# Laying out a kernel's on-chip buffers by class: weights at multiples of 128 bytes, streamed operands 64 bytes off

## The chip, the core and the metric

The kernel runs on one core of a Trainium2 chip. The core has a matrix engine (PE), a vector engine (DVE), a scalar engine (ACT), a general engine (POOL), a queue engine that issues the loads (SP), and 16 DMA engines. On-chip memory has 128 partitions; a tile is a range of bytes that is the same in every partition, so a tile's place is one byte address. The metric is device time of one launch in microseconds (us).

## What is computed

A two-layer decoder trunk on 256 positions of width 1024, batch 1, all in float32: a recurrent block and a gated feed-forward block (FFN), then a shared key/value projection, causal attention with 8 heads and a second FFN. Each block has a root-mean-square norm and a shift and scale that are computed from `c`.

```python
def swiglu(h, w_gate, w_up, w_down):
    return (jax.nn.silu(h @ w_gate) * (h @ w_up)) @ w_down

x = x + g_m[:, None, :] * rglru_mixer(h, ...)      # layer 0
x = x + g_f[:, None, :] * swiglu(h, ...)
x = x + g_m[:, None, :] * moba_mixer(h, ...)       # layer 1
x = x + g_f[:, None, :] * swiglu(h, ...)
return rmsnorm(x, final_norm)
```

`D_FF` is 2816, so each FFN has 2 x 176 weight blocks of 128 x 128 for gate and up and 176 for down.

## The kernel before

The weights come in units of up to 128 x 2048 float32, one DMA each, into a `raw` tile. A matrix product is not done in plain float32. Each weight unit is split in two parts of the matrix engine's rounded float32 type: ACT copies `raw` into `whi` (L433), DVE subtracts that from `raw` into `wlo` (L434). The activations are split in the same way into `..._h` and `..._l`. `mm3` then records three matmuls per 128 x 128 block, at L381 (high weights, high activations), L382 (high weights, low activations) and L383 (low weights, high activations). The weight block is the operand that is loaded into the array ahead of a matmul (the trace's PEld), and the activation block, 128 x 256, is the one that streams through it.

In the FFN the first product (`f_p`) has a unit of 16 weight blocks, 48 matmuls, and streams the four pairs of tiles `f_h` and `f_l`, each with two blocks of 256 columns. The second product (`f_d`) streams eleven pairs `f_ah` and `f_al`. The first two blocks of gate and up (`f_g`) are computed ahead of the norm from tiles `f_u_h` and `f_u_l` with 258 columns; in the first FFN they are done in plain float32 (L443), in the second by three matmuls. The products of the recurrent block (`yb`, `wo`), the query and output products of the attention (`qp`, `ao`) are made like `f_p`. The value product (`vp`) has the two roles exchanged: there the weights stream, 512 columns wide, and the activations are loaded.

All tiles that live for a while only are kept in slots. A class has a fixed number of slots of one size: `t1` 18 of 1032 bytes, `t2` 32 of 2048 bytes, `raw`, `whi` and `wlo` 4 each of 8192 bytes, `mraw` 3 of 4096 bytes. Every streamed operand of `mm3` but those with 258 columns (`t1`) is in a `t2` slot. A planner (`Plan.run`) orders the instructions of every engine from costs and ranks that are written in the code, and gives each tile a slot as its first user is placed. The pool places a slot (a tag) in memory when a tile of that tag is asked for the first time, behind all that was placed until then, and each later tile of the tag has the same place. So before, the slots of all classes lie mixed, in the order in which the plan first used them. Since a `t1` slot has 1032 bytes, taken as 1056, each `t1` slot moves what follows by 32 bytes modulo 128.

Of the kernel before, what the change touches and what calls it, by code (L numbers as in the profile page):

```python
# [12 lines left out]
F32 = mybir.dt.float32  # L13
# [5 lines left out]
P = 128  # L19
D = 1024  # L20
S = 256
# [18 lines left out]
CU = 2048  # L40
# [52 lines left out]
class Plan:  # L93
# [175 lines left out]
KN = {  # L269
    "sp": 287, "winf": 400, "conv": 84, "ga": 109, "y": 284, "ypsum": 80, "ex": -650, "rec": -97, "ge": 245,  # L270
    "gm": 181, "wo": 221, "scf": 103, "shf": -189, "x1": 0, "split": 4, "swp": 1178.2266785918575, "scat": 5,
    "shat": 0, "gmat": 1, "win": 600, "tol": 3.6321997149340305e-16, "nn": 5, "nyh": 1, "sqpe": 1, "gnat": 5,
    "fnat0": 1, "md": "sc", "rawn": 4, "wn": 4, "t2n": 32, "t2r": 2,
}
# [37 lines left out]
T1N, T2N, RAWN, WN, MRN = 18, KN["t2n"], KN["rawn"], KN["wn"], 3  # L312
# [5 lines left out]
def build(tc, t):  # L318
    nc = tc.nc
    ctx = ExitStack()  # L320
    with ctx:
        pool = ctx.enter_context(tc.tile_pool(name="sb", bufs=1))
        psum = ctx.enter_context(tc.tile_pool(name="ps", bufs=1, space=bass.MemoryType.PSUM))
        ctx.enter_context(tc.manual_schedule())
        pl = Plan()
        TW = S + 2

        def slots(cls, n, w, reserve=None, pool=pool):

            pl.slots(cls, n, lambda b, i: pool.tile([P, w], b.dt, name=f"{cls}_{b.name}", tag=f"{cls}{i}"), reserve)  # L330

        slots("t1", T1N, TW, 6)
        slots("t2", T2N, 2 * S, KN["t2r"])
        slots("raw", RAWN, CU, None)
        slots("whi", WN, CU)
        slots("wlo", WN, CU)
        slots("mraw", MRN, D)
        slots("ps", 8, 512, 2, psum)

        def own(shape, name):  # L340
# [208 lines left out]
        def normed(xk, rstd, name):  # L549
            n = T1(name)  # L550
            tt(S, lambda: nc.vector.tensor_mul(n.ap[:, :S], xk.ap[:, :S], rstd.ap[:, :S]), (xk, rstd), (n,))
            return n

        def to_h(n, a, sh, abuf, h, j, name):

            f = T1(name)
            act(S, lambda: nc.scalar.activation(f.ap[:, :S], n.ap[:, :S], AF.Identity, bias=sh(), scale=a()),
                (n,) + abuf, (f,), aps=2)
            hi, lo = h
            o = j * S  # L560
            act(S, lambda: nc.scalar.activation(hi.ap[:, o:o + S], f.ap[:, :S], AF.Copy), (f,), ((hi, o),))
            tt(S, lambda: nc.vector.tensor_sub(lo.ap[:, o:o + S], f.ap[:, :S], hi.f[:, o:o + S]), (f, (hi, o)),
               ((lo, o),))
            return f
# [85 lines left out]
        for k in range(KC):  # L650
# [10 lines left out]
            f = to_h(normed(x0[k], rstd0, f"n0_{k}"), lambda k=k: sc0.ap[:, k:k + 1], lambda k=k: sh0.ap[:, k:k + 1],  # L661
                     ((sc0, k), (sh0, k)), h0[k // 2], k % 2, f"h0_{k}")
# [309 lines left out]
        for k in range(KC):  # L972
            n = normed(x2[k], rstd2, f"n2_{k}")
# [256 lines left out]
```

## Time and profile before

| what | value |
|---|---|
| time, median of 3 runs | 629.61 us (628.73 to 631.35) |
| the profiled execution: time | 628.5 us |
| its span, first to last instruction | 626.7 us |
| PE busy | 597.9 us, 95% of the span |
| DVE busy | 472.6 us, 75% |
| ACT busy | 338.0 us, 54% |
| HBM read | 161.14 MB, 259 GB/s over the span |

The span and the time differ by 1.8 us, which lie around the instructions. Shares are means over stages with different limits, so they say little about one stage. Matmuls overlap: one matmul is shown with 283 ns from start to end, while the next one starts 120 ns after it. What a row of matmuls costs is therefore read from the distance of their starts, not from the mean of one.

### The profile page before, as it was taken

Reading aid. Unit: us, or ns where it says so; the run is one execution under the profiler, and the core shown is the slowest. Engines: PE = TensorE matmul, PEld = TensorE weight load, DVE = VectorE, ACT = ScalarE, POOL = GpSimd, SP = SyncE. Lnnn points to the kernel's source line nnn. Section 1 sums busy time; section 2 is a strip of 40 time slices with the busy share of each in tenths; the row PEclk is TensorE's granted clock in tenths of the full one; section 3 lists DMA queues with packets and bytes.
Section 4 is the critical chain, followed back from the end, with each engine's and each line's share of the span. In section 5 each row is a group of like instructions: output and inputs, shape, how many; then the busy total and the mean of one; then the engine's idle time right before and its main releaser. Section 6 shows DMA issues by size and latency. Waiting matters only on the chain.

```text
span 626.7 us, 11500 instructions
## 1 busy us (share of the span) xinstructions
PE 597.9 (95%) x4688; PEld 574.6 (92%) x4688; DVE 472.6 (75%) x718; ACT 338.0 (54%) x485; POOL 35.1 (6%) x68
## 2 busy tenths in 40 slices
PE   3999899998999999999997999997999999999996
PEld 1899778997999999999996999997999999999996
DVE  6898978887988789988756789888997555545542
ACT  5537998627653444253444988766555433333322
POOL 0000000032000000001006000006000000000000
PEclk9999999999999999999998999998999999999999
DMA  8886897687988899998878248885686543445501
GB/s 292 327 339 241 318 391 302 257 319 291 415 311 306 317 332 355 326 332 333 321 282 318 75 164 315 302 315 215 224 319 226 195 174 132 139 145 186 180 1 68
DMA packets 33363, 162.95 MB, mean 260 GB/s; under 512 B 3700, under 2 KB 4893, under 8 KB 23966
## 3 DMA queue, kind: packets, MB, share of 16 engines
q1 hardware_dynamic: 33310, 162.21, 70.1%
q8 instruction: 37, 0.61, 0.4%
q14 instruction: 16, 0.13, 0.1%
HBM read 161.14 MB, written 1.06 MB: 259 GB/s over the span
## 4 chain that ended last, share of the span: by engine, by line
PE 81%; DVE 6%; DMA 5%; issue 2%; ACT 2%; POOL 2%; SPq 0%; DVEq 0%; POOLq 0%; ACTq 0%
PE ps_f_p L382 12%; PE ps_f_p L381 12%; PE ps_f_p L383 12%; PE ps_f_d L382 7%; PE ps_f_d L381 6%; PE ps_f_d L383 6%; PE ps_xb L670 2%; DVE t_xc L702 2%; PE ps_f_g L443 2%; PE ps_yb L381 1%; PE ps_yb L382 1%; DMA raw_sh_f_r<-in_modp 1%; PE ps_qp L382 1%; PE ps_qp L381 1%; PE ps_qp L383 1%
## 5 line engine op out<-in xcount | busy, mean ns | idle before, releaser
L382 PE MATMUL ps_f_p<-t_f_l,whi_f0b_h 128*128 128x256 f32 x320 | 90.6, 283 | 0.0
L381 PE MATMUL ps_f_p<-t_f_h,whi_f0b_h 128*128 128x256 f32 x320 | 90.5, 283 | 0.0
L383 PE MATMUL ps_f_p<-t_f_h,wlo_f0b_l 128*128 128x256 f32 x320 | 90.3, 282 | 0.0
L381 PE MATMUL ps_f_p<-t_f_h,whi_f1b_h 128*128 128x256 f32 x320 | 90.2, 282 | 0.0
L383 PE MATMUL ps_f_p<-t_f_h,wlo_f1b_l 128*128 128x256 f32 x320 | 90.1, 282 | 0.0
L382 PE MATMUL ps_f_p<-t_f_l,whi_f1b_h 128*128 128x256 f32 x320 | 90.1, 282 | 0.0
L434 DVE TENSOR_TENSOR wlo_f1b_l<-raw_f1b_r,whi_f1b_h 128x2048 fp32r<-128x2048 f32 x20 | 45.8, 2289 | 21.7 <-ACT whi_f1b_h L433 21.5
L381 PEld LDWEIGHTS ps_f_p<-t_f_h,whi_f0b_h 128*128 128x128 f32 x320 | 61.1, 191 | 0.0
L382 PEld LDWEIGHTS ps_f_p<-t_f_l,whi_f0b_h 128*128 128x128 f32 x320 | 61.1, 191 | 0.0
L383 PEld LDWEIGHTS ps_f_p<-t_f_h,wlo_f0b_l 128*128 128x128 f32 x320 | 61.1, 191 | 0.0
L382 PEld LDWEIGHTS ps_f_p<-t_f_l,whi_f1b_h 128*128 128x128 f32 x320 | 60.8, 190 | 0.0
L381 PEld LDWEIGHTS ps_f_p<-t_f_h,whi_f1b_h 128*128 128x128 f32 x320 | 60.8, 190 | 0.0
L383 PEld LDWEIGHTS ps_f_p<-t_f_h,wlo_f1b_l 128*128 128x128 f32 x320 | 60.8, 190 | 0.0
L433 ACT ACTIVATE whi_f1b_h<-raw_f1b_r 128x2048 fp32r<-128x2048 f32 x20 | 38.1, 1913 | 27.1 <-issue 19.3
L434 DVE TENSOR_TENSOR wlo_f0b_l<-raw_f0b_r,whi_f0b_h 128x2048 fp32r<-128x2048 f32 x20 | 45.7, 2289 | 9.0 <-ACT whi_f0b_h L433 8.9
L433 ACT ACTIVATE whi_f0b_h<-raw_f0b_r 128x2048 fp32r<-128x2048 f32 x20 | 38.1, 1911 | 22.2 <-issue 19.1
L382 PE MATMUL ps_f_d<-t_f_al,whi_f1c_h 128*128 128x256 f32 x176 | 49.8, 283 | 0.0
L381 PE MATMUL ps_f_d<-t_f_ah,whi_f0c_h 128*128 128x256 f32 x176 | 49.7, 282 | 0.0
L381 PE MATMUL ps_f_d<-t_f_ah,whi_f1c_h 128*128 128x256 f32 x176 | 49.6, 282 | 0.0
L382 PE MATMUL ps_f_d<-t_f_al,whi_f0c_h 128*128 128x256 f32 x176 | 49.6, 282 | 0.0
L383 PE MATMUL ps_f_d<-t_f_ah,wlo_f1c_l 128*128 128x256 f32 x176 | 49.6, 282 | 0.0
L383 PE MATMUL ps_f_d<-t_f_ah,wlo_f0c_l 128*128 128x256 f32 x176 | 49.6, 282 | 0.0
(470 smaller groups left out, 1696.7 us busy)
## 6 DMA issues: line engine op xcount, KB each, us to landing
raw_f0b_r<-in_ffb SPq DMA_DIRECT2D x20, 1024.0 KB, 6.0
raw_f1b_r<-in_ffb SPq DMA_DIRECT2D x20, 1024.0 KB, 5.9
raw_f0c_r<-in_ffc SPq DMA_DIRECT2D x16, 704.0 KB, 6.5
raw_f1c_r<-in_ffc SPq DMA_DIRECT2D x16, 704.0 KB, 4.1
raw_wix<-in_win_x SPq DMA_DIRECT2D x8, 768.0 KB, 7.2
raw_wout_r<-in_wout SPq DMA_DIRECT2D x5, 1024.0 KB, 8.5
raw_wiy_r<-in_win_y SPq DMA_DIRECT2D x4, 1024.0 KB, 7.5
raw_sh_f_r<-in_modp SPq DMA_DIRECT2D x4, 1024.0 KB, 8.3
```

The lines of the kernel that those rows point to most:

```text
L381: nc.tensor.matmul(o, h_, a_, start=start, stop=False, skip_group_check=skip)
L382: nc.tensor.matmul(o, h_, b_, start=False, stop=False, skip_group_check=skip)
L383: nc.tensor.matmul(o, l_, a_, start=False, stop=stop, skip_group_check=skip)
L433: act(n - o, lambda: nc.scalar.activation(hi.ap[:, o:n], raw.ap[:, o:n], AF.Copy), (raw,), (hi,))
L434: tt(n - o, lambda: nc.vector.tensor_sub(lo.ap[:, o:n], raw.ap[:, o:n], hi.f[:, o:n]), (raw, hi), (lo,))
L443: pe(n * 0.0016875 + 0.002, lambda: nc.tensor.matmul(ps.ap[:, c:c + n], lo.ap[:, o:o + w], xh.ap[:, xo:xo + n], start=start, stop=stop, sk ...
L670: pe(0.432, lambda k=k, m=m, c=c, ps=ps, wr=wr, f=f: nc.tensor.matmul(ps.ap[:, c:c + S], wr.ap[:, m * P:(m + 1) * P], f.ap[:, :S], start=( ...
L702: stt(S, lambda m=m, j=j, o=o, tap=tap: nc.vector.scalar_tensor_tensor(x_.ap[:, o], xv()[:, j, tap:tap + S], V("cw", tap * 10 + m), x_.ap[ ...
```

## The change

The slots are placed before anything else, class by class, and the tiles that stay for the whole program follow. For that, `slots` asks the pool once for a tile of each tag; these tiles have no instruction. A tile of 64 bytes, named `shift`, is placed between `mraw` and `t2`.

```diff
         def slots(cls, n, w, reserve=None, pool=pool):
 
             pl.slots(cls, n, lambda b, i: pool.tile([P, w], b.dt, name=f"{cls}_{b.name}", tag=f"{cls}{i}"), reserve)
-
-        slots("t1", T1N, TW, 6)
-        slots("t2", T2N, 2 * S, KN["t2r"])
-        slots("raw", RAWN, CU, None)
+            if pool is not psum:
+                for i in range(n):
+                    pool.tile([P, w], F32, name=f"{cls}_home{i}", tag=f"{cls}{i}")
+
+
         slots("whi", WN, CU)
         slots("wlo", WN, CU)
+        slots("raw", RAWN, CU, None)
         slots("mraw", MRN, D)
+        pool.tile([P, 16], F32, name="shift", tag="shift")
+        slots("t2", T2N, 2 * S, KN["t2r"])
+        slots("t1", T1N, TW, 6)
         slots("ps", 8, 512, 2, psum)
```

In the two built programs every engine has the same instructions in the same order, with the same waits; only line numbers (5 more below the edit) and buffer numbers differ. What differs is where the tiles lie:

| class | address modulo 128, before | now |
|---|---|---|
| `whi` (4 slots) | one at 96, three at 0 | 0 |
| `wlo` (4) | 0 | 0 |
| `raw` (4) | one at 64, three at 0 | 0 |
| `mraw` (3) | 64, 96, 64 | 0 |
| `t2` (32) | three at 64, 29 at 0 | 64 |
| `t1` (18) | 0, 32, 64 or 96 | each as before |
| tiles that stay | 0, 32, 64 or 96 | each as before |

Which tile has which slot is the same in both. Modulo 512 the weight blocks and the streamed blocks have these places: before, the 29 slots and all weight slots but one are at 384, so that the two are 0 apart; now the weights are at 128 and the streamed blocks at 192, so that a weight block lies 64 below its streamed block (448 modulo 512).

Two places in the program are needed further down. In the matrix engine's order, a part of a unit of the second FFN's first product before: `f1_h3` is one of the few streamed tiles in a slot at 64 modulo 128, the others here are at 0, and so are the weights.

```order
L382 MATMUL ps_f1_p31_5348<-t2_f1_l2_5077,whi_f1b31_h_5189 128x256
L383 MATMUL ps_f1_p31_5348<-t2_f1_h2_5055,wlo_f1b31_l_5236 128x256
L381 MATMUL ps_f1_p31_5348<-t2_f1_h3_5079,whi_f1b31_h_5189 128x256
L382 MATMUL ps_f1_p31_5348<-t2_f1_l3_5096,whi_f1b31_h_5189 128x256
L383 MATMUL ps_f1_p31_5348<-t2_f1_h3_5079,wlo_f1b31_l_5236 128x256
```

Nothing moves there; now all these streamed tiles are at 64. The second place is in the products with 258 columns at the start of the second FFN, whose streamed tiles are in `t1` slots. Here the high part `u3_h` is at 448 modulo 512 and the low part `u3_l` at 320, and both weight blocks at 384.

```order
L383 MATMUL ps_f1_g01_4805<-t1_f1_u3_h_4859,wlo_f1a0_l_4705 128x258
L381 MATMUL ps_f1_g02_4810<-t1_f1_u3_h_4859,whi_f1a0_h_4552 128x258
L382 MATMUL ps_f1_g02_4810<-t1_f1_u3_l_4871,whi_f1a0_h_4552 128x258
L383 MATMUL ps_f1_g02_4810<-t1_f1_u3_h_4859,wlo_f1a0_l_4705 128x258
L381 MATMUL ps_f1_g03_4814<-t1_f1_u3_h_4859,whi_f1a0_h_4552 128x258
```

Nothing moves there either, and the `t1` tiles keep their places modulo 128.

## Rows read from the trace of the kernel before

**Rows 1.** The page's chain of work that ended last, shares by engine.

```profile
PE 81%; DVE 6%; DMA 5%; issue 2%; ACT 2%; POOL 2%; SPq 0%; DVEq 0%; POOLq 0%; ACTq 0%
```

**Rows 2.** Busy time by stretch: two of first FFN, attention, two of second FFN.

```profile
core 0: us, PE busy (x) PEld busy (x) DVE busy (x) ACT busy (x) POOL busy (x), PEclk, DMA share, GB/s
156.40:271.50 115.10, 115.10 (x962) 115.06 (x961) 102.31 (x134) 53.63 (x55) 0.00 (x0) 1.00 0.91 336
271.50:330.60 59.10, 59.10 (x498) 58.97 (x497) 43.98 (x53) 23.72 (x21) 2.75 (x3) 1.00 0.86 323
354.00:424.00 70.00, 70.00 (x519) 66.72 (x518) 62.52 (x136) 55.18 (x120) 1.79 (x3) 1.00 0.71 264
442.00:555.30 113.30, 113.30 (x957) 113.30 (x956) 71.90 (x76) 51.48 (x52) 0.00 (x0) 1.00 0.55 197
555.30:618.80 63.50, 63.50 (x536) 63.50 (x534) 30.39 (x35) 22.23 (x23) 0.00 (x0) 1.00 0.34 113
```

**Rows 3.** Groups of instructions: count, then busy us, mean ns, idle before.

```profile
L382 PE MATMUL ps_f_p<-t_f_l,whi_f0b_h 128*128 128x256 f32 x320 | 90.6, 283 | 0.0
L382 PE MATMUL ps_f_d<-t_f_al,whi_f0c_h 128*128 128x256 f32 x176 | 49.6, 282 | 0.0
L381 PE MATMUL ps_ao<-t_oh,whi_wo_h 128*128 128x256 f32 x64 | 18.7, 292 | 0.0
```

**Rows 4.** Timeline of PE (start, us): first matmuls of two successive first-FFN units.

```profile
185.38 0.28 PE L381 MATMUL ps_f_p<-t_f_h,whi_f0b_h 128*128 128x256 f32 x1
...
191.14 0.28 PE L381 MATMUL ps_f_p<-t_f_h,whi_f0b_h 128*128 128x256 f32 x1
```

**Rows 5.** Timeline of PE: second FFN, matmuls with 258 columns.

```profile
435.01 0.28 PE L383 MATMUL ps_f_g<-t_f_u_h,wlo_f1a_l 128*128 128x258 f32 x1
435.13 0.28 PE L381 MATMUL ps_f_g<-t_f_u_h,whi_f1a_h 128*128 128x258 f32 x1
435.24 0.28 PE L382 MATMUL ps_f_g<-t_f_u_l,whi_f1a_h 128*128 128x258 f32 x1
435.37 0.28 PE L383 MATMUL ps_f_g<-t_f_u_h,wlo_f1a_l 128*128 128x258 f32 x1
435.48 0.28 PE L381 MATMUL ps_f_g<-t_f_u_h,whi_f1a_h 128*128 128x258 f32 x1
435.60 0.28 PE L382 MATMUL ps_f_g<-t_f_u_l,whi_f1a_h 128*128 128x258 f32 x1
435.72 0.28 PE L383 MATMUL ps_f_g<-t_f_u_h,wlo_f1a_l 128*128 128x258 f32 x1
```

**Rows 6.** Timeline of PE: second FFN, first product, two pieces.

```profile
472.32 0.29 PE L381 MATMUL ps_f_p<-t_f_h,whi_f1b_h 128*128 128x256 f32 x1
...
473.26 0.28 PE L383 MATMUL ps_f_p<-t_f_h,wlo_f1b_l 128*128 128x256 f32 x1
...
481.61 0.28 PE L381 MATMUL ps_f_p<-t_f_h,whi_f1b_h 128*128 128x256 f32 x1
...
487.24 0.28 PE L381 MATMUL ps_f_p<-t_f_h,whi_f1b_h 128*128 128x256 f32 x1
```

**Rows 7.** Pieces of the chain that ended last: start us, us, what.

```profile
29.51 2.16 PE ps_xb L670 x10
...
129.77 6.49 DMA mraw_mr_sc_f_m__1416<-in_mod
...
354.45 0.23 PE ps_vp L381
```

**Rows 8.** Timeline of DVE, then of PE, near the first FFN's end.

```profile
305.44 1.63 DVE L434 TENSOR_TENSOR wlo_f0c_l<-raw_f0c_r,whi_f0c_h 128x1408 fp32r<-128x1408 f32 x1 [0.48 <-ACT whi_f0c_h L433]
307.45 1.62 DVE L434 TENSOR_TENSOR wlo_f0c_l<-raw_f0c_r,whi_f0c_h 128x1408 fp32r<-128x1408 f32 x1 [0.38 <-ACT whi_f0c_h L433]
...
310.80 0.28 PE L381 MATMUL ps_f_d<-t_f_ah,whi_f0c_h 128*128 128x256 f32 x1
```

**Rows 9.** Waits of ACT from 157 to 330 us: total us, times, longest.

```profile
ACT whi_f0c_h L433 <- DMA raw_f0c_r<-in_ffc: 15.9, 6, 4.4
```

## The prediction

> **What bounds the kernel now.** I read the chain of work first: 81% of the span is PE, no other engine has over 6% [rows 1]. Then the stretches of the trace one by one. In five of them, 421 us together, PE is busy without a gap: 115.10 of 115.10 us, 59.10 of 59.10 and so on [rows 2]. These are the two FFNs and the attention, and in them only the spacing of the matmuls and what feeds PE can matter. DVE is busy 102.31 of 115.10 us in the worst of them and the DMA engines 91%, so neither is at its limit, though both are near it in the first FFN and far from it in the second (71.90 of 113.30 us, and 55%). [...]
>
> A matmul's own duration (283 ns, [rows 3]) is no price, since the next one starts long before it ends. So I take the time between starts. In a unit of the first FFN in which the streamed tiles and all weights are at 0 modulo 128, the 48 matmuls from one unit's first to the next unit's first take 191.14 - 185.38 = 5.76 us, 120.0 ns each [rows 4]. The weight loads fill that time too: PEld is busy 115.06 of 115.10 us [rows 2]. So while one block streams, the next block's weights are read, all the time, from the same memory.
>
> **Does the place matter? Three stretches.** The kernel before has a few tiles elsewhere, so its trace is a small experiment. (a) The piece of the second FFN in which `f1_h3` (at 64) is streamed, with its neighbours at 0: eight steps from 472.32 to 473.26 us, 0.94 us, 117.5 ns each, against 120.0 [rows 6]. (b) A unit of that product whose high weights lie at 96 and which streams `f1_h3` twice: 487.24 - 481.61 = 5.63 us for 48, 117.3 ns [rows 6]. (c) The matmuls with 258 columns on `u3`, the nearest to what the change makes, because there the loaded weights lie 64 below the streamed tile (384 against 448 modulo 512) as all of them will now. The two steps during which the high part streams take 435.24 - 435.01 = 0.23 us and, one cycle later, 435.60 - 435.37 = 0.23 us: 115 ns each. The step during which the low part streams (weights 64 above it) takes 0.13 and 0.12 us. All six take 0.71 us, 118.3 ns [rows 5]. The timeline rounds to 0.01 us, so the 115 is good to some 5 ns.
>
> I conclude that places decide some nanoseconds per matmul, and that the distance of 0 is the worst that occurs over a long stretch: neither (a), (b) nor (c) is above 120 in the mean.
>
> [...]
>
> **The change part by part.** No instruction, wait or queue entry is added, removed or moved, so every term is a duration.
>
> *Matmuls of three with a `t2` tile streaming.* Per FFN, 3 x 320 of `f_p` and 3 x 176 of `f_d`: 1488 [rows 3]. The attention has 3 x 64 for `ao` and as many for `qp`: 384. Now the spacing: a window's count holds about two matmuls that only reach into it, so in the first FFN 115.10 us / 960 = 119.9 ns and 59.10 / 496 = 119.2, together 119.7; in the second 113.30 / 955 = 118.6 and 63.50 / 534 = 118.9, together 118.7 [rows 2]. For the new spacing the ends are 125 ns, the long step of (c), and 108 ns, half of the 216 ns that a plain float32 pass over 256 columns takes (2.16 us for ten, [rows 7]); that the rounded type takes half as long when nothing disturbs it is an estimate. Between them I take 115 ns, the step of (c) at the new distance. First FFN: (119.7 - 115) x 1488 = 7.0 us. Second: (118.7 - 115) x 1488 = 5.5 us. Attention: 4.2 x 384 = 1.6 us, of which I count half, 0.8 us: there DVE is busy 62.52 of 70 us and each head waits for its exponentials. Sum 13.3 us.
>
> *The same matmuls ahead of the first FFN* (`yb`, `wo` and part of `xb`, about 600 matmuls): 0 us. They are covered by loads: the chain goes through a DMA of 6.49 us at 129.77 us, after most of them [rows 7]. Without that cover they would give 600 x 4.5 = 2.7 us.
>
> *What feeds PE in the first FFN.* When PE is faster, weight slots come free earlier and ACT, DVE and SP move up with it, unless the loads are at their limit. In this FFN ACT waits for `raw_f0c` 15.9 us in six waits [rows 9]. The tightest unit has its low weights ready at 305.44 + 1.63 = 307.07 us and its first matmul at 310.80 us [rows 8]: 3.7 us of reserve. By then PE has gained (310.80 - 156.40) / 0.1197 x 4.7 ns = 6.1 us. If no load came earlier, 2.4 us of the gain would be lost; if all did, nothing. DMA is 91% and 86% busy, not full, so I take 0.9 us. What is late next in that case is a `wlo` at the start of a unit of `f_d`. The second FFN has no such limit at 55% and 34% DMA.
>
> *ACT and DVE on other addresses.* Nothing: DVE's split takes 1.63 us in a unit with high weights at 0 and 1.62 us in the next, where they are at 96 [rows 8]. *`vp`*: here weights stream and `t2` tiles are loaded, so the sign of the distance is turned round; a matmul takes 0.23 us for 512 columns [rows 7], and 48 of them change by 0.8 us at most if one goes to the 216 ns of [rows 7] or as far the other way. *`raw` and `mraw` at 0* are places that DMAs write; 0 us, since the FFNs with most of PE's time do not wait for them except as costed above.
>
> Sum: 13.3 - 0.9 = 12.4 us. 628.5 - 12.4 = 616.1 us in the terms of the profiled execution; the median of the runs stands 0.2% above that execution, so 617 us.
>
> **The rivals.**
>
> *Give-back.* The short steps of (c) and the 0.11 to 0.12 us around them may be paid by the long ones: two operands that change their distance drift, and one at a constant distance settles at the mean, some 117.5 ns as in (a) and (b). For it: in (c) 115 never stands alone for more than two steps. Gain (119.2 - 117.5) x 3360 = 5.7 us: 624 us.
>
> *Nothing happens.* The reads are independent, or they fall into step at any constant distance, as they do at 0, where every step of a unit is 0.12 us. Against it: (a) to (c). 629 us, within 3 us. [...]
>
> *Slower.* All matmuls settle in the long step. Place: both FFNs and the attention; price: 125 ns instead of 119.2, 5.8 x 3360 = 19 us, 649 us. It decides as soon as the settled step is above 119.2 ns. For it speaks only that long steps occur at all at a distance of 64, with the other sign; against it that at the new sign four of four steps are about 115.
>
> *More than expected.* The two reads no longer meet at all: 108 ns, (119.2 - 108) x 3360 = 38 us less, less what the first FFN's loads hold back. For it speaks nothing seen; half way, at 112 ns, it would be about 606 us.
>
> **How the numbers follow.** 115 ns and its surroundings (113 to 117): 0.56, 610 to 622 us. Give-back: 0.19. Nothing: 0.13. Slower: 0.06. More: 0.06. The range from 608 to 627 us holds the first two and the edges of "nothing" and "more", about 8 in 10. A measurement of this kernel tells 0.5% (3 us) from no change; the limit is 626.5 us. Faster: 0.56 + 0.06 + nearly all of give-back, 0.80. Same: 0.14. Slower: 0.06.
>
> **What would show it.** In the trace of the changed kernel, 48 matmuls of a unit of `f_p` should take 5.52 us (115 ns each) instead of 5.76, in all units alike, since all distances are equal; the windows of the second FFN should be shorter by some 5.5 us together, with PE still without a gap. The two passes of the split on ACT and DVE should take what they take now. In the first FFN a wait of PE for `wlo_f0c` would show that the loads hold back the gain. A step that stays at 0.12 us throughout makes the prediction wrong in its first term, a step of 0.12 to 0.13 in its sign. A shorter step with an unchanged time would mean that I misread what PE waits for.

## The result, and the profile after

The changed kernel takes 622.93 us (median of 6 executions, 621.48 to 626.17), the kernel before 629.28 us (median of 6 on the same chip). The ratio is 0.9906, with an interval from 0.9885 to 0.9927. The forecast was 617 us with a range from 608 to 627: the direction came out, and about half of the size, 6.4 us by the medians (5.9 by the ratio) instead of 12.4. Here and below a ratio leaves out an execution that lies more than 1.5% above the fastest of its kernel; there are two, in e8_hilo128 and e10_again.

The profiled execution took 623.06 us, with a span of 621.2 us. First the page's chain by engine, then three of its groups of instructions (count, busy us, mean ns, idle before), which answer to [rows 1, 3]:

```profile
PE 80%; ACT 6%; DVE 4%; DMA 4%; POOL 2%; issue 2%; SPq 0%; DVEq 0%; POOLq 0%; ACTq 0%
...
L387 PE MATMUL ps_f_p<-t_f_l,whi_f0b_h 128*128 128x256 f32 x320 | 89.4, 279 | 0.0
L439 DVE TENSOR_TENSOR wlo_f0b_l<-raw_f0b_r,whi_f0b_h 128x2048 fp32r<-128x2048 f32 x20 | 45.7, 2289 | 8.3 <-ACT whi_f0b_h L438 8.3
...
L387 PE MATMUL ps_f_d<-t_f_al,whi_f0c_h 128*128 128x256 f32 x176 | 49.1, 279 | 0.0
```

PE is the chain as before, and a matmul's own duration has gone from 283 and 282 to 279 ns, which is no price. The same stretches as in [rows 2] (busy us and count of each engine, granted clock, DMA share, GB/s):

```profile
core 0: us, PE busy (x) PEld busy (x) DVE busy (x) ACT busy (x) POOL busy (x), PEclk, DMA share, GB/s
156.40:271.50 115.10, 115.10 (x978) 115.07 (x978) 102.75 (x136) 53.68 (x53) 0.00 (x0) 1.00 0.89 333
...
442.00:555.30 113.30, 113.30 (x964) 113.30 (x963) 71.03 (x73) 50.00 (x50) 0.00 (x0) 1.00 0.55 194
```

PE has no gap (115.10 of 115.10 us) and the granted clock is 1.00, as before, and more matmuls fit into the same time: 978 for 962, 964 for 957. The price is in the starts. The timeline of PE, the first matmul of two units in the first FFN and of two in the second:

```profile
182.94 0.28 PE L386 MATMUL ps_f_p<-t_f_h,whi_f0b_h 128*128 128x256 f32 x1
...
188.59 0.28 PE L386 MATMUL ps_f_p<-t_f_h,whi_f0b_h 128*128 128x256 f32 x1
...
471.83 0.28 PE L386 MATMUL ps_f_p<-t_f_h,whi_f1b_h 128*128 128x256 f32 x1
...
477.49 0.28 PE L386 MATMUL ps_f_p<-t_f_h,whi_f1b_h 128*128 128x256 f32 x1
```

48 matmuls take 5.65 and 5.66 us, where [rows 4] have 5.76 and the forecast had 5.52. That is 117.8 ns each. The program's order tells which weight unit a matmul of the trace belongs to: in all 76 units that PE ran through without a break (30 to 48 matmuls, the first six steps left out) the mean step is 117.7 or 117.8 ns. So the term "matmuls of three" was worth (119.7 - 117.8) x 1488 = 2.8 us in the first FFN and (118.7 - 117.8) x 1488 = 1.3 us in the second, not 7.0 and 5.5. (By [rows 2] the 119.7 is rather 119.6, which is 0.1 us of the sum.)

One place of the same trace showed that this is not the whole story. The timeline of PE in the first FFN, around a step of 0.13 us and a break of 0.22 us:

```profile
157.52 0.28 PE L387 MATMUL ps_f_p<-t_f_l,whi_f0b_h 128*128 128x256 f32 x1
157.64 0.29 PE L388 MATMUL ps_f_p<-t_f_h,wlo_f0b_l 128*128 128x256 f32 x1
157.77 0.28 PE L386 MATMUL ps_f_p<-t_f_h,whi_f0b_h 128*128 128x256 f32 x1
157.88 0.28 PE L387 MATMUL ps_f_p<-t_f_l,whi_f0b_h 128*128 128x256 f32 x1
...
158.11 0.28 PE L386 MATMUL ps_f_p<-t_f_h,whi_f0b_h 128*128 128x256 f32 x1
158.22 0.38 PE L387 MATMUL ps_f_p<-t_f_l,whi_f0b_h 128*128 128x256 f32 x1
158.44 0.28 PE L388 MATMUL ps_f_p<-t_f_h,wlo_f0b_l 128*128 128x256 f32 x1
158.56 0.28 PE L386 MATMUL ps_f_p<-t_f_h,whi_f0b_h 128*128 128x256 f32 x1
```

From 157.77 to 158.22 us four steps take 0.45 us, 113 ns each, behind a step of 0.13; then a start comes 0.22 us after the last one, and from there on it is 117.8 ns. The tiles stand at the same distance all the time.

### The profile page after: what moved, and what is told of

The parts are those of the page before. It is cut to its first block, busy times and chain, and to the rows that moved or that the text cites. A ratio compares the mean times of both kernels' runs of the same rounds, so it can differ in the third digit from the quotient of the medians.

```text
span 621.2 us, 11500 instructions
## 1 busy us (share of the span) xinstructions
PE 593.1 (95%) x4688; PEld 569.8 (92%) x4688; DVE 471.9 (76%) x718; ACT 338.1 (54%) x485; POOL 34.9 (6%) x68
## 4 chain that ended last, share of the span: by engine, by line
PE 80%; ACT 6%; DVE 4%; DMA 4%; POOL 2%; issue 2%; SPq 0%; DVEq 0%; POOLq 0%; ACTq 0%
PE ps_f_p L388 12%; PE ps_f_p L386 12%; PE ps_f_p L387 12%; PE ps_f_d L388 6%; PE ps_f_d L386 6%; PE ps_f_d L387 6%; PE ps_xb L675 2%; PE ps_f_g L448 2%; PE ps_yb L386 1%; PE ps_yb L388 1%; PE ps_yb L387 1%; PE ps_qp L388 1%; PE ps_qp L386 1%; PE ps_qp L387 1%; DMA mraw_mr_sc_f_m__1482<-in_mod 1%
```

## The experiments

All kernels are the changed kernel with other places for the slots; the work is the same. I call distance the address of the weights being loaded minus that of the tile that streams, modulo 512; the changed kernel has 448 throughout, that is -64. The trace doesn't show addresses: the distances are those of the places that the program gives to the tiles. By these places one of the 29 slots that the section on the change has at 384 modulo 512 before lies at 256, which is 0 modulo 128 too; of the distances that are 0 modulo 128, the experiments have 0 alone. Each kernel leaves out the `shift` tile and puts tiles without an instruction in front of the slots, by a table of bytes:

```diff
             if pool is not psum:
                 for i in range(n):
+                    if any(PADS.get(cls, ())[i:i + 1]):
+                        pool.tile([P, PADS[cls][i] // 4], F32, name=f"{cls}_pad{i}", tag=f"{cls}_pad{i}")
                     pool.tile([P, w], F32, name=f"{cls}_home{i}", tag=f"{cls}{i}")
...
-        pool.tile([P, 16], F32, name="shift", tag="shift")
```

**e1_flat: the order by class alone, distance 0 throughout.**

```diff
+        PADS = {}
```

> Slots class by class as in the changed kernel, but without the 64 bytes ahead of t2: all weights and all streamed tiles at 0 modulo 128, distance 0 everywhere. Theory A (the spacing is settled by the constant distance of loaded weights and streamed tile): 120.0 ns in every unit of both FFNs, also in those that had 117 to 119 before; 48 matmuls in 5.76 us; time 629 to 632 us, 1% above the changed kernel. Theory B (the placing by class itself, or the alignment of raw and mraw, gave the gain): about 623 us and a spacing below 120. The recurrent part tells more: under A the first FFN starts at 139.5 us as before the change, under B at 137.5 as after it.

Measured: 630.97 us (10 executions), a ratio of 1.0024 to the kernel before, interval 1.0005 to 1.0042. The first matmuls of two successive units of the first FFN, timeline of PE:

```profile
182.61 0.28 PE L387 MATMUL ps_f_p<-t_f_h,whi_f0b_h 128*128 128x256 f32 x1
...
188.37 0.28 PE L387 MATMUL ps_f_p<-t_f_h,whi_f0b_h 128*128 128x256 f32 x1
```

5.76 us for 48, and 119.9 or 120.0 ns in all 76 units without a break. The order by class and the multiples of 128 alone bring no gain; it takes the 64 bytes. One sign of theory B is there all the same: the first FFN starts at 137.58 us, as in the changed kernel (137.45) and not as before (139.55). And 1.6 us of this trace are not the step: from 137 to 157 us the granted clock is 0.91 in the mean, where the changed kernel has 1.00, and the time from the first matmul of `f_g` to that of `f_p` is 18.57 instead of 16.94 us.

**e2_dist32: distances of 0, 32, 64 and 96, one for each pair of weight slots.**

```diff
+        PADS = {'whi': (0, 32, 32, 32), 'wlo': (416, 32, 32, 32), 'raw': (416, 0, 0, 0)}
```

> One trace with four constant distances: the four slot pairs of whi and wlo lie 0, 32, 64 and 96 bytes above the streamed tiles (modulo 512), so that successive units of f_p have these distances in turn. Theory A: each unit settles in a spacing of its own: 120.0 ns at 0, about 118 at 64, 32 and 96 between 116 and 119. Theory C (any distance but 0 gives the same): 117.8 in the three others.

Measured: 625.69 us (one execution). In the FFNs, units at 0 have 119.8 to 120.0 ns. At 32 they have 118.1 to 118.3, with steps from 115 to 123 that repeat. At 96 eleven of 17 have 117.3 to 117.5, one has 118.5, and five have 120.0, among them all four of the first FFN's second product. At 64 there are two values, 117.8 in five units and 113.3 in twelve. Here are the starts of a unit at 64 and of the next, first in the first FFN and then in the second:

```profile
183.28 0.28 PE L387 MATMUL ps_f_p<-t_f_h,whi_f0b_h 128*128 128x256 f32 x1
...
188.94 0.28 PE L387 MATMUL ps_f_p<-t_f_h,whi_f0b_h 128*128 128x256 f32 x1
...
475.12 0.28 PE L387 MATMUL ps_f_p<-t_f_h,whi_f1b_h 128*128 128x256 f32 x1
...
480.58 0.28 PE L387 MATMUL ps_f_p<-t_f_h,whi_f1b_h 128*128 128x256 f32 x1
```

5.66 us and 5.46 us, 117.8 and 113.3 ns (the last unit's 5.46 holds the step into the next distance), with the same distance. So the distance alone doesn't set the step, and neither theory comes out whole. The streamed tiles lie as in e1_flat here, at 0 modulo 128, and only the weights are moved. That 64 gives 117.8 ns this way round too speaks against a rival that e1_flat leaves open, that the place of the streamed tiles by itself decides.

**e3_dist128 and e5_dist128_timed: distances of 448, 64, 192 and 320, all 64 modulo 128.** The two are the same kernel; the second was timed in several executions.

```diff
+        PADS = {'whi': (448, 128, 128, 128), 'wlo': (128, 128, 128, 128), 'raw': (192, 0, 0, 0)}
```

> Four distances that are all 64 modulo 128 but differ modulo 512: 448 (as in the changed kernel), 64, 192 and 320. Theory A with a period of 128 bytes: 117.8 ns in every unit. Theory D (higher address bits or the sign matter, which would explain steps of 115 and 124 ns at plus and minus 64 before): units differ by more than 1 ns, with 64 above 448.

> The kernel of e3 (slot pairs 448, 64, 192 and 320 bytes above the streamed tiles, modulo 512), now timed. Theory H (at 64 modulo 128 the same addresses have two settled steps, 113.3 and 117.8 ns; a stretch that starts in the long one stays there until something disturbs it, and a change of the distance by 128 is such a disturbance): 113.3 ns in nearly all of both FFNs in every execution, 611 to 615 us, ratio 0.972 to 0.978. Theory R (which step is taken is chance at each start): times on several levels between 612 and 624 us.

Measured: 612.92 us, then 612.64 us (6 executions, 611.63 to 614.32), a ratio of 0.9729 to the kernel before, interval 0.9705 to 0.9753. In both traces 67 of the 68 units of the FFNs have 113.3 ns, at every one of the four distances. Here, from e3, are the start of a unit at 448 and that of the next, 5.44 us later:

```profile
172.15 0.28 PE L387 MATMUL ps_f_p<-t_f_h,whi_f0b_h 128*128 128x256 f32 x1
...
177.59 0.28 PE L387 MATMUL ps_f_p<-t_f_h,whi_f0b_h 128*128 128x256 f32 x1
```

That refutes a settled step that belongs to 448, and leaves two readings: a change of distance helps while it lasts, or it tips the row of matmuls into another state that then stays.

**e4_mixed: high and low weights at different distances (0 and 64, 32 and 96).**

```diff
+        PADS = {'whi': (0, 32, 32, 32), 'wlo': (480, 32, 416, 32), 'raw': (480, 0, 0, 0)}
```

> High and low weights of a unit at different distances: 0 and 64, 32 and 96, 64 and 0, 96 and 32 bytes above the streamed tile in the four slot pairs, so that the distance changes within each three matmuls. Theory A: the mean of the two constant distances, weighted two to one, about 118 to 119 ns. Theory E (a change of distance breaks the settled step and gives short steps of 115 that are not paid back): below 117.8 in the mean.

Measured: 624.46 us (one execution), 117.7 to 118.0 ns in all 68 units of the FFNs, although each three changes its distance twice. A change between 64 and 0 or between 32 and 96 does not bring the short step; theory E is refuted, and the mean of theory A is missed where 0 is one of the two distances (120.0 and 117.8, weighted, would be 118.5 to 119.3).

**e6_const320: one distance throughout, 320 instead of 448.**

```diff
+        PADS = {'t2': (192,)}
```

> All weights 320 above the streamed tiles modulo 512, constant, as the changed kernel has 448. Theory H: like the changed kernel, 117.8 ns where a stretch starts so, with 113.3 only behind a break; 620 to 625 us. Theory D (bits above 7 decide, and 448 alone is bad): 113.3 ns in all units, 611 to 615 us.

Measured: 620.53 us (4 executions, 617.40 to 621.88), ratio 0.9846, interval 0.9813 to 0.9879. In the trace, that of the execution with 617.40 us, the first FFN runs at 113.3 ns until a break of 1.1 us at 299.95 us and at 117.8 behind it, and the second FFN at 117.8. One distance, two steps.

**e7_one128: one of the four pairs of weight slots moved by 128.** Three units in four keep 448, the fourth has 64.

```diff
+        PADS = {'whi': (128, 384, 0, 0), 'wlo': (128, 384, 0, 0), 't2': (64,)}
```

> The changed kernel with one of the four slot pairs moved by 128 bytes (distance 448 in three pairs, 64 in one). Theory H: 117.8 ns at the start of an FFN, 113.3 from about the first unit with the moved pair on, and it stays at 113.3 through the units with 448: 612 to 616 us. Theory D: one unit in four at 113.3, the others at 117.8, about 620 us.

Measured: 613.04 us (4 executions, 610.29 to 615.52), ratio 0.9731, interval 0.9692 to 0.9771. Timeline of PE in the first FFN: the first start of an ordinary unit, some starts of the next, which has the moved pair, and the first starts of the two ordinary units behind it:

```profile
166.78 0.28 PE L387 MATMUL ps_f_p<-t_f_h,whi_f0b_h 128*128 128x256 f32 x1
...
171.73 0.28 PE L387 MATMUL ps_f_p<-t_f_h,whi_f0b_h 128*128 128x256 f32 x1
171.84 0.28 PE L388 MATMUL ps_f_p<-t_f_l,whi_f0b_h 128*128 128x256 f32 x1
171.97 0.28 PE L389 MATMUL ps_f_p<-t_f_h,wlo_f0b_l 128*128 128x256 f32 x1
172.09 0.28 PE L387 MATMUL ps_f_p<-t_f_h,whi_f0b_h 128*128 128x256 f32 x1
172.20 0.28 PE L388 MATMUL ps_f_p<-t_f_l,whi_f0b_h 128*128 128x256 f32 x1
172.31 0.28 PE L389 MATMUL ps_f_p<-t_f_h,wlo_f0b_l 128*128 128x256 f32 x1
...
177.19 0.28 PE L387 MATMUL ps_f_p<-t_f_h,whi_f0b_h 128*128 128x256 f32 x1
...
182.63 0.28 PE L387 MATMUL ps_f_p<-t_f_h,whi_f0b_h 128*128 128x256 f32 x1
```

Until 171.73 us the unit's 42 matmuls take 4.95 us, 117.9 ns each. Then the distance changes, three steps take 0.36 us together (171.73 to 172.09), from there they are 113 ns, and PE waits for nothing. The unit from 177.19 us on is back at 448 and keeps 113.3 ns (5.44 us for 48), and so does all that follows in this FFN, with one exception: in `f0_d5`, at 301.7 us, PE breaks off for 1.3 us, goes on at 117.8 ns, and is at 113.3 again from the place where the distance changes the next time. The second FFN tells the same: 117.7 ns until 451.07 us, the first unit with the moved pair, and 113.3 from there to the end. The short step outlasts the change that brought it.

**e8_hilo128: high weights at 448, low weights at 64.** The distance changes twice in each three.

```diff
+        PADS = {'wlo': (128, 0, 0, 0), 'raw': (384, 0, 0, 0), 't2': (64,)}
```

> The changed kernel with all low weights 128 bytes further (distance 448 for high, 64 for low weights), so that the distance changes by 128 twice in each three matmuls. Theory H: the long step never lasts; 113.3 ns from the start of every stage, the short products of the attention too; 610 to 614 us, a little below e5. Theory A in its first form (each constant distance has one step, 117.8): as the changed kernel, 623 us.

Measured: 616.11 us (6 executions, 611.85 to 622.70; 614.55 without the longest), ratio 0.9768, interval 0.9725 to 0.9811. I had expected that no long step lasts; that was a miss. Units of the first FFN and of the second, in an execution of 619.64 us:

```profile
189.32 0.28 PE L387 MATMUL ps_f_p<-t_f_h,whi_f0b_h 128*128 128x256 f32 x1
...
195.03 0.28 PE L387 MATMUL ps_f_p<-t_f_h,whi_f0b_h 128*128 128x256 f32 x1
...
473.79 0.28 PE L387 MATMUL ps_f_p<-t_f_h,whi_f1b_h 128*128 128x256 f32 x1
...
479.23 0.28 PE L387 MATMUL ps_f_p<-t_f_h,whi_f1b_h 128*128 128x256 f32 x1
```

5.71 us and 5.44 us: 118.9 ns through the first FFN (one step in six is 124) and 113.3 through the second. The distances inside each three are 448, 448 and 64, the sequence of [rows 5], and there is again a pair of settled steps; a stretch stays in the one it came into. So a change of distance between matmuls does not always lead to the short step: what brought it in e7_one128 was one change between long rows of equal distance.

**e9_alternate and e10_again: distances by turns, and the changed kernel itself once more.** e10_again has no edit; the table of e9_alternate is

```diff
+        PADS = {'whi': (0, 128, 384, 128), 'wlo': (384, 128, 384, 128), 'raw': (384, 0, 0, 0), 't2': (64,)}
```

> Weight slots by turns at a distance of 64 and 448 modulo 512 below the streamed tiles, so that the distance changes by 128 from unit to unit throughout. Theory H (at 64 modulo 128 there are two settled steps, 113.3 and 117.8 ns, and a change of distance by 128 between units leaves the long one but not the short one): nearly all units of the two FFNs at 113.3 ns and 612 to 614 us, as with four distances and with one moved pair. Rival (the short step came from particular distances, 192 or 320 below, or from few changes): a good part of the units at 117.8 ns, 617 to 623 us.

> The changed kernel itself once more. Theory H: each stretch of equal units settles at 117.8 or at 113.3 ns, nothing between; if the way in decides it the same way each time, all units at 117.8 and 621 to 626 us; if it is open from run to run, some stretches at 113.3 and single times down to 613 us. Rival (117.8 ns is the only step at a distance of 448): all units at 117.8 ns in every run, no time below 620 us.

Measured for e9_alternate: 612.64 us (4 executions, 610.98 to 613.03), ratio 0.9730, interval 0.9698 to 0.9763, with 113.3 ns in every unit of both FFNs but the last of the first. (In the second FFN the plan gives pairs of successive units the same distance, so there it changes with every second unit.) Measured for e10_again: 624.91 us (7 executions, 617.47 to 629.50), ratio 0.9939, interval 0.9904 to 0.9974. Its profiled execution, though, took 617.47 us, the only one below 622. Its first FFN, at a break like the one above, and then the first starts of units of the first and of the second FFN:

```profile
153.18 0.28 PE L386 MATMUL ps_f_p<-t_f_h,whi_f0b_h 128*128 128x256 f32 x1
...
156.12 0.36 PE L387 MATMUL ps_f_p<-t_f_l,whi_f0b_h 128*128 128x256 f32 x1
156.32 0.28 PE L388 MATMUL ps_f_p<-t_f_h,wlo_f0b_l 128*128 128x256 f32 x1
156.44 0.28 PE L386 MATMUL ps_f_p<-t_f_h,whi_f0b_h 128*128 128x256 f32 x1
156.55 0.28 PE L387 MATMUL ps_f_p<-t_f_l,whi_f0b_h 128*128 128x256 f32 x1
156.66 0.28 PE L388 MATMUL ps_f_p<-t_f_h,wlo_f0b_l 128*128 128x256 f32 x1
...
179.90 0.28 PE L386 MATMUL ps_f_p<-t_f_h,whi_f0b_h 128*128 128x256 f32 x1
...
185.34 0.28 PE L386 MATMUL ps_f_p<-t_f_h,whi_f0b_h 128*128 128x256 f32 x1
...
466.29 0.28 PE L386 MATMUL ps_f_p<-t_f_h,whi_f1b_h 128*128 128x256 f32 x1
...
471.94 0.28 PE L386 MATMUL ps_f_p<-t_f_h,whi_f1b_h 128*128 128x256 f32 x1
```

The steps are near 118 ns up to 156.12 us, then one start comes 0.20 us after the last, and behind it they are 113.3 ns (5.44 us for 48) up to the first FFN's last unit, ahead of which PE breaks off for 0.9 us. In the second FFN they are 117.8 (5.65 us). This is the same program as the one whose other trace has 117.8 ns everywhere: the step is not a property of the addresses alone, and here a break tipped it the other way than in the first trace. Of 13 executions of this program it alone took less than 621 us.

The traces of e3, e5, e7 and e9 together show more closely what tips a row. A change from 448 to 64 between two units without a break met a row in the long step seven times, four of them in e7_one128, and each time the row went on in the short one. Three other changes met a long row and left it long: from 64 to 448 in e7_one128 (112.85 us) and from 320 to 64 in e3 and e5 (408.87 and 409.23 us). A row in the short step kept it over every change of distance without a break in these four traces.

The profiled executions fall on levels by how many FFNs had the short step:

| 113.3 ns in | kernel | profiled execution |
|---|---|---|
| neither FFN | changed kernel | 623.06 us |
| most or nearly all of the first | e6_const320, e10_again | 617.40, 617.47 us |
| the second | e8_hilo128 (118.9 in the first) | 619.64 us |
| nearly all of both | e3 and e5, e7, e9 | 612.92 to 613.26 us |

An FFN has 1488 such matmuls, and (117.8 - 113.3) x 1488 = 6.7 us. With the first FFN alone 5.6 us were gained, with both 10 us. By the stages in the table further down, e9_alternate gains 6.3 us on the changed kernel in the first FFN and 5.5 in the second; it comes to the first FFN 0.9 us later and takes 0.9 us longer for the attention.

## Why the prediction was half right

*The cause, and the direction: right.* The change acts by the distance of the loaded weights from the streamed tile. e1_flat, with the same order of classes and a distance of 0, has 120.0 ns and no gain; in e2_dist32, weights moved against the same streamed tiles move the step (119.8 to 120.0 ns at 0, 117.8 or 113.3 at 64). With equal instructions the step is 120.0, 117.8 or 113.3 ns.

*The step that failed: "Between them I take 115 ns, the step of (c) at the new distance".* The term was mis-sized: 117.8 ns were measured, in both FFNs. The 115 ns of [rows 5] is no settled step. There the distance changes inside each three, and short steps stand beside steps of 0.12 to 0.13 us. When e7_one128 changes its distance, steps of up to 0.13 us come in the same way, before the step settles. e8_hilo128, with the same sequence of distances for whole FFNs, settles at 118.9 or 113.3 ns and not at 115. Nor were the four steps of 115 typical: the twelve steps at a distance of 448 in that stretch of the trace before, by the places in the program, have 117.0 ns in the mean. What [rows 5] could tell was the mean, 118.3 ns, and [rows 6] had 117.5 and 117.3: the three rows agree within 1 ns with what came. I averaged where I wanted direction and picked a single step where I wanted size. A premise failed with it, that equal distances give one step "in all units alike": at the changed kernel's own distance e10_again has 113.3 and 117.8 ns.

*Give-back: right in the number, not in its reason.* It said 117.5 ns and 624 us. It also said that a constant distance settles at the mean of short and long steps. But the changed kernel's own second trace runs at 113.3 ns at its constant distance through most of an FFN. There are two settled steps, and 117.8 is the one that this kernel mostly comes into. That [rows 6], at other distances, had nearly this number was luck in part.

*Nothing* is excluded by the interval (0.9885 to 0.9927) and by e1_flat's 120.0 against 117.8, *slower* by the same numbers: the longest settled step seen is 120.0 ns. *More* (108 to 112 ns, the 108 an estimate that no run shows) was never reached, but 113.3 ns and 612.6 us were, by the kernels that tip it.

*Loads that hold back the first FFN, 0.9 us: not there in the changed kernel, but there in others with the short step.* No wait of PE for `wlo_f0c` stands in the changed kernel's trace, nor in those of e5, e9_alternate and e10_again, where PE runs faster. In e3, e6_const320 and e7_one128 the forecast sign came, 0.3, 0.8 and 1.0 us; in the last two it is in the break that threw PE back to 117.8 ns. First the wait of e7_one128 (us in total, times, longest):

```profile
PE ps_f_d L389 <- DVE wlo_f0c_l L440: 1.0, 1, 1.0
```

In the changed kernel ACT waits for the loads somewhat longer than in [rows 9], and this stays hidden:

```profile
ACT whi_f0c_h L438 <- DMA raw_f0c_r<-in_ffc: 17.0, 8, 4.4
```

*ACT and DVE on other addresses, nothing: right.* ACT's copies of the weights of the first FFN's second product take 1380 ns in the mean in both traces, and DVE's split takes what it took in [rows 8]:

```profile
301.40 1.62 DVE L439 TENSOR_TENSOR wlo_f0c_l<-raw_f0c_r,whi_f0c_h 128x1408 fp32r<-128x1408 f32 x1
303.32 1.63 DVE L439 TENSOR_TENSOR wlo_f0c_l<-raw_f0c_r,whi_f0c_h 128x1408 fp32r<-128x1408 f32 x1 [0.30 <-ACT whi_f0c_h L438]
```

*Ahead of the first FFN 0, attention 0.8 us, second FFN 5.5 us: by stages.* From the first matmul of each stage in the traces, in us:

| stage | before | changed | changed, second trace | e9_alternate |
|---|---|---|---|---|
| up to the first FFN's first matmul | 139.55 | 137.45 | 135.40 | 138.34 |
| first FFN up to `f_d` | 132.00 | 130.29 | 126.10 | 126.16 |
| its `f_d`, and the norm behind it | 63.72 | 63.12 | 60.93 | 60.92 |
| attention | 88.49 | 87.97 | 88.99 | 88.87 |
| second FFN, its norm and up to `f_d` | 131.51 | 131.80 | 133.67 | 128.71 |
| its `f_d` | 63.75 | 62.90 | 62.90 | 60.54 |

Of the 5.4 us between the profiled executions of the two kernels, 2.3 came in the first FFN, 0.5 in the attention, 0.6 in the second FFN, and 2.1 ahead of the first FFN, where I had forecast none. The last does not follow the step: e1_flat, with 120.0 ns throughout, comes to the first FFN at 137.58 us, and two executions of the changed kernel lie 2.05 us apart there. All eleven traces with slots by class come there between 135.40 and 138.34 us, ahead of the 139.55 before, so some of the 2.1 us may belong to the order by class; with one trace of the kernel before this is not shown. The second FFN's front differs by 1.9 us between the two traces of one program, both at 117.8 ns: there PE waits for POOL 3.3 us in the first and 5.3 us in the second, and why stays open.

*What stays open.* What makes two steps at one distance, and what a stretch has to meet in order to come into the shorter one: a break did it in both directions, a change from 448 to 64 between units only ever towards the short one, as far as the traces here show. At 96 too a distance had two steps, 117.3 and 120.0 ns in e2_dist32. Whether the spread of the single times (621.48 to 626.17 us here, 617.47 to 625.72 in e10_again without its longest) comes from this too was not shown, since only one execution of each run has a trace.

## What to carry to other kernels

In these runs, where every matmul loads its own weights (978 matmuls beside 978 loads in the changed kernel's first stretch) and PE has no gap (115.10 of 115.10 us there), the distance of the loaded from the streamed tile was worth 2 to 6% of the time of the matmuls (117.8 and 113.3 ns against 120.0 at 0). So try a distance other than 0, and read what it gives from the mean over whole units, never from single steps. At a distance of 64 modulo 128, giving one of the four pairs of weight slots or more a distance that is 128 off (e3 and e5, e7, e9) was worth another 1.6%: 612.6 us instead of 622.9. Take two traces of one program before a time per step is called that of a layout.

## What was not expected of the hardware

With equal instructions, equal addresses and the granted clock at 1.00, rows of matmuls with 256 columns and a load of 128 ran at either 113.3 or 117.8 ns from start to start, for more than 160 us on end, and changed between the two within a few matmuls at a break of 0.2 us or at a change of distance. A distance of 0 had one step, 119.9 to 120.0 ns in 76 of 76 units of e1_flat.
